# Transposing the residual before its norm is known: the step between the output projection and the feed-forward half of a decoder block

## The chip, the cores and the metric

The kernel runs on one core of one Trainium2 chip. The time is device time in microseconds (us) of one execution on that core, a median over several runs. A core has TensorE (PE, matrix products into PSUM), VectorE (DVE), ScalarE (ACT), GpSimd (POOL) and a queue engine (SP) that issues the loads. Each engine works through its own instructions in order.

## The reference, cut to what matters

One layer of a decoder trunk, 256 tokens, width 2048, feed-forward width 5632, all in float32. The part around the change:

```python
x = x + g1 * y                                       # y: the mixers' outputs @ w_out
h = rmsnorm(x, norm_ffn) * (1.0 + sc2) + sh2         # sc2, sh2: one number for each of the 2048 features
gate = causal_dwconv(h @ w_gate, conv_w) + conv_b
x = x + g2 * ((silu(gate) * (h @ w_up)) @ w_down)
# rmsnorm(x, w) = x * rsqrt(mean(x * x, axis=-1) + 1e-6) * w
```

## The kernel before

Every float32 product of the large matrices is made of three products of rounded parts: a value is split into a high part (`wh`, `Y2[:, k, 0:T]`, `H2[:, k, 0:T]`; ScalarE casts) and a low part (`wl`, the second half of `Y2` or `H2`; VectorE subtracts). Weights come by pieces of 128x1024 (512 KB): a load into one of five buffers `wr`, then the split into one of three buffers `wh` and `wl` (L158). A piece's buffers come free when TensorE is done with it. The order of the instructions on each engine is not written by hand: a scheduler takes the program's order as priority and lets a later instruction go ahead where, by its own model of the times, the earlier ones can't start yet.

**End of the attention half.** The output projection (`project`, L950) works through five chunks of columns; for each of the two token tiles `t` of 128 it sums into one PSUM bank `wot`. Each chunk is then multiplied by the gate `g1` (`m_`, L984), added to the residual `x1` (in the trace: bigC; L985), and squared on ScalarE with a sum by token (`x1s`, L986). In the trace helpers have one line each: L97 is every product (transposes have lines of their own), L100 every two-input VectorE operation, L103 scalar_tensor_tensor, L107 and L109 tensor_scalar, L112 ScalarE's activation, L115 the cast of a split.

**Start of the feed-forward half.** The sums `x1s` give the factor by token `s1` (L996 to L998, the power on GpSimd), and two diagonal matrices `dg` hold it (L1000). For each of 16 tiles `k` of 128 features, two float32 products `x1` times `dg` transpose the residual and scale it by token at once (L1005), into one of eight PSUM banks `fpt`; ScalarE applies scale and shift by feature (`h2`, in the trace h, two buffers; L1007); then the split into `H2` (in the trace bigA; L1008).

**The gate and up projections** (`proj`, L1014) take four `fpt` banks at a time; over the 16 `k` they add, for each of four column tiles, a 512-column product with `wh` and a 256-column product with `wl`. Eleven pairs of such blocks, then the product with `w_down`, fill the rest of the kernel.

Of the kernel before, what the change touches and what calls it, by code (L numbers as in the profile page):

```python
# [16 lines left out]
P = 128  # L17
# [11 lines left out]
# columns of w_in  # L29
# [3 lines left out]
# columns of the constant array  # L33
# [11 lines left out]
# the groups of K tiles in which w_in is worked through: first tile, how many  # L45
GROUPS = ((0, 4), (4, 4), (8, 4), (12, 4))
NG = len(GROUPS)
# how many of the 18 pairs of columns beside DeltaNet's queries, keys and values each group but the last visits
TAKE = (16, 12, 11)
# the order of the mixers: gla, pooling, forgetting attention, DeltaNet  # L50
ORDER = "gpfd"
# modulations (s: scale 2, h: shift 2, g: gate 1; half) summed on the tensor engine and on VectorE, steps per load of columns
# [4 lines left out]
def _consts():  # L57
    i = np.arange(P)
    s, t = i[:, None], i[None, :]
    same = (s // CH) == (t // CH)  # L60
    cols = [s == t, same & (s <= t), same & (s > t), s <= t, np.ones((P, P)), s > t]
    cols.append(np.where(t > s, -1e30, 0.0))
    for w in (2, 4, 8, 16):
        cols.append(np.broadcast_to(1.0 / np.minimum(np.arange(1, 17), w), (P, 16)))
    # the level at which s and t part, counted from 1 above the diagonal and from 7 below it
    lv = sum((l + 1) * ((s // (2 * m) == t // (2 * m)) & (s % (2 * m) < m) & (t % (2 * m) >= m))
             for l, m in enumerate(LEVELS))
    lw = lv.T
    cols.append(lv + np.where(lw > 0, lw + len(LEVELS), 0))
    return np.ascontiguousarray(np.concatenate([np.asarray(a, np.float32) for a in cols], axis=1))  # L70
# [3 lines left out]
def trunk_kernel(ctx: ExitStack, tc: tile.TileContext, x, c, w_mod, b_mod, norm_mix, norm_ffn, w_in,  # L74
# [21 lines left out]
    def mm(o, l, r, start=True, stop=True):  # L96
        PE.matmul(o, lhsT=l, rhs=r, start=start, stop=stop, skip_group_check=True)  # L97
# [30 lines left out]
    # ones in the rows 0 and 64, and in the rows 32 and 96  # L128
# [45 lines left out]
    def gemv(col0, done, pst=None, ready=lambda: True, bias=None):  # L174
        """cond * w over 1024 columns: without pst summed by partition on VectorE, else on the tensor engine,
        four column tiles side by side"""
        acc = pst() if pst else keep.tile([P, 1024], F32, name="ga", tag="ga")
        if bias is not None:
            G.memset(acc, 0.0)
            nc.sync.dma_start(acc[0:1], bias)  # L180
        for k in range(0, KT, 2):
            wms = []
            for kk in range(2):
                wms.append(wp.tile([P, 1024], F32, name="wm", tag="wm", bufs=4))
                last_wm[0] = nc.sync.dma_start(wms[kk], wm_v[:, k + kk, col0:col0 + 1024])
            for kk in range(2):
                wm = wms[kk]
                if not pst:
                    accumulate(acc, wm, k + kk, bias is None)
                    continue  # L190
                for c in range(2):
                    o = 64 * kk + 32 * c
                    mm(acc[o:o + 32], cond[:, k + kk:k + kk + 1].to_broadcast([P, 32]), wm[:, c * 512:c * 512 + 512],
                       start=k == 0, stop=k == KT - 2)
            if k == KT - 2:
                while not ready():
                    yield
                with tc.high_priority():
                    if pst:
                        gr = wp.tile([P, 1024], F32, name="wr", tag="wr", bufs=5)[:, 0:512]  # L200
                        S_.copy(gr, acc)
                        done([(gr, sel[:, c:c + 1]) for c in range(2)])
                    else:
                        done([(acc[:, c * 512:c * 512 + 512], ones) for c in range(2)])
            yield
# [21 lines left out]
    # ================= attention half =================  # L227
    with ExitStack() as ph:
# [11 lines left out]
        # projections: gla q 0:2, k 2:4, g 4:8, gdn g 8:12, pool 12:16, fox q 16:20, k 20:24  # L240
# [16 lines left out]
        def gates():  # L257
# [13 lines left out]
            # columns 0:4 1/(1+e), columns 4:12 1/(2+e)  # L271
# [16 lines left out]
        with ExitStack() as st:  # L288
# [25 lines left out]
            # 1 + b_mod of the two scales  # L314
# [19 lines left out]
            # sh1, sc1 of the K tiles of group g, then h  # L334
# [60 lines left out]
            # the small columns: lr 0:16, b 16:20, a 20:24, f 24:28; row 28 is one  # L395
# [30 lines left out]
            # one pair of column tiles over some groups of K tiles; two sums share a bank: only the first clears it  # L426
# [68 lines left out]
            # g1 takes the place of values no longer needed  # L495
# [33 lines left out]
            # conv of gdn's q, k, v straight from the accumulators  # L529
# [37 lines left out]
        def gated_deltanet():  # L567
            # norms of q and k
# [12 lines left out]
            # decays within the chunk  # L581
# [17 lines left out]
            for t in range(NT):  # L599
                ts = slice(t * P, t * P + P)  # L600
                # exp of the decays, transposed: [j, i], i no earlier than j
# [8 lines left out]
                # -M^T (and its diagonal, which no level takes)  # L610
# [9 lines left out]
            # inverse of I + M by blocks of 2, 4, .. 64: X = inverse, Y = its transpose  # L620
# [30 lines left out]
            for t in range(NT):  # L651
                ts = slice(t * P, t * P + P)
                # keys and values by token
# [9 lines left out]
                # attention [j, i]  # L663
# [5 lines left out]
                # queries times the decay from the chunk's start  # L669
# [6 lines left out]
            # u and w^T, over the values' and the keys' place  # L676
# [10 lines left out]
            # the states, chunk by chunk, over M and X  # L687
# [19 lines left out]
            # outputs, normalised, in place of Y  # L707
            oss, ors = dt_("oss", zz), dt_("ors", zz)
            for t in range(NT):
# [12 lines left out]
                # r = c * (c^2 * ss / d + eps)^-1/2  # L722
# [9 lines left out]
        def finish(on_t, t, nw, i, b):  # L732
            """the gate's place takes the gated output, [features, tokens]"""
            for h in range(4):
                PE.transpose(b[:, h], on_t[:, h], ident)
            o = pr[:, i:i + 4, t * P:t * P + P]
            stt(o, b, nw, o, ALU.mult, ALU.mult)

# [1 line left out]
        def gla(lp):  # L740
# [4 lines left out]
            # log decays by token, then their sums within the chunk by feature  # L745
# [14 lines left out]
            # attention within the chunk, [s, t], heads by parity: the diagonal, then level by level  # L760
# [29 lines left out]
            # to and from the states  # L790
# [159 lines left out]
        def project(n, a):  # L950
            c0, w = chunks[n]
            nk = 1024 // w
            for j in range(KT // nk):
                ks = order[nk * j:nk * j + nk]
                if n == 0:
                    for k in ks:
                        split(Y2[:, k, 0:T], Y2[:, k, T:], pr[:, k + 4])
                wh, wl = load_split(wo_v, ks[0], nk, c0, w)
                for kk, k in enumerate(ks):
                    st, sp_ = j + kk == 0, nk * j + kk == KT - 1  # L960
                    for t in range(NT):
                        xh, xl = Y2[:, k, t * P:t * P + P], Y2[:, k, T + t * P:T + t * P + P]
                        mm(a[t], xh, wh[:, kk], start=st, stop=False)
                        mm(a[t], xh, wl[:, kk], start=False, stop=False)
                        mm(a[t], xl, wh[:, kk], start=False, stop=sp_)
# [22 lines left out]
    # ================= feed-forward half =================  # L988
    with ExitStack() as ph:
# [3 lines left out]
        with tc.tile_pool(name="hp", bufs=2, reuse_waits="tile") as hp:  # L993
            s1 = hp.tile([P, 4], F32, name="s1", bufs=1)
            dg = hp.tile([P, NT, P], F32, name="dg", bufs=1)
            V.tensor_reduce(out=s1[:, 0:2], in_=x1s, axis=AX.X, op=ALU.add)  # L996
# [4 lines left out]
            # transposed and scaled by the norm in one product  # L1001
            for k in range(KT):
                b = fpt()
                for t in range(NT):
                    mm(b[:, t * P:t * P + P], x1[:, t, k * P:k * P + P], dg[:, t])  # L1005
                h = hp.tile([P, T], F32, name="h2", tag="h2", bufs=2)
                act(h, b[:, 0:T], AF.Identity, scale=s2[:, k:k + 1], bias=sh2[:, k:k + 1])  # L1007
                split(H2[:, k, 0:T], H2[:, k, T:], h)  # L1008
# [5 lines left out]
        def proj(gp, view, c0):  # L1014
            """four column tiles, weights stationary: [features, tokens], the high and the low part's sums side by side"""
# [29 lines left out]
        # down: tokens stationary; g2 and the final norm's weight by row  # L1045
# [72 lines left out]
```

## Time and profile before

| | us |
|---|---|
| median of 3 runs | 1316.04 |
| lowest and highest | 1313.96, 1318.38 |
| span of the profiled execution, from its first to its last instruction | 1312.4 |
| TensorE busy in it | 1257.7 (96%) |
| VectorE busy | 886.8 (68%) |
| ScalarE busy | 640.7 (49%) |
| end of the last product of the output projection | 540.54 |
| start of the first product of the gate's projection | 556.71 |

The page tells the profiled execution by its span alone. Times in the trace are us from the span's start. A busy TensorE is not TensorE at its peak: its products are pipelined, their recorded ends overlap the next ones, and its clock has two levels, which the page gives as the granted clock (1.00 is 2.4 GHz, 0.50 is 1.2 GHz).

### The profile page before, as it was taken

Reading aid. Unit: us, or ns where it says so; the run is one execution under the profiler, and the core shown is the slowest. Engines: PE = TensorE matmul, PEld = TensorE weight load, DVE = VectorE, ACT = ScalarE, POOL = GpSimd, SP = SyncE. Lnnn points to the kernel's source line nnn. Section 1 sums busy time; section 2 is a strip of 40 time slices with the busy share of each in tenths; the row PEclk is TensorE's granted clock in tenths of the full one; section 3 lists DMA queues with packets and bytes.
Section 4 is the critical chain, followed back from the end, with each engine's and each line's share of the span. In section 5 each row is a group of like instructions: output and inputs, shape, how many; then the busy total and the mean of one; then the engine's idle time right before and its main releaser. Section 6 shows DMA issues by size and latency. Waiting matters only on the chain.

```text
span 1312.4 us, 20435 instructions
## 1 busy us (share of the span) xinstructions
PE 1257.7 (96%) x7955; PEld 1100.5 (84%) x7955; DVE 886.8 (68%) x1185; ACT 640.7 (49%) x1008; POOL 23.1 (2%) x31
## 2 busy tenths in 40 slices
PE   2799999999999999899999999999999999999996
PEld 1799999898876788888888888888888888888896
DVE  7688797989763497456656665665666587974553
ACT  3455344674364444465545455554555454443432
POOL 0200000010000100000000000000000000000000
PEclk8799999999999999899999999999999999999998
DMA  9999998796567996345565565555655699875552
GB/s 332 287 368 376 312 353 279 259 334 211 176 233 247 328 338 230 125 161 186 170 206 180 189 190 183 190 184 187 191 184 172 206 356 378 304 260 188 192 182 81
DMA packets 174232, 311.95 MB, mean 238 GB/s; under 512 B 16172, under 2 KB 65331, under 8 KB 173495
## 3 DMA queue, kind: packets, MB, share of 16 engines
q1 hardware_dynamic: 174135, 310.65, 70.3%
q8 instruction: 62, 1.02, 0.3%
q14 instruction: 35, 0.29, 0.1%
HBM read 308.51 MB, written 2.10 MB: 237 GB/s over the span
## 4 chain that ended last, share of the span: by engine, by line
PE 91%; DMA 4%; DVE 1%; SPq 1%; ACT 1%; issue 1%; POOLq 0%; POOL 0%; ACTq 0%; DVEq 0%
PE fpt L97 57%; PE ext L97 15%; PE wot L97 5%; PE acc L97 4%; PE gdt L97 4%; PE bgt L97 3%; DMA wm<-in_w_mod_dram 3%; PE oxt L97 2%; DMA wr<-in_w_in_dram 1%; DMA wr<-in_w_out_dram 1%; DVE ga L103 1%; DVE wl L100 0%; ACT h L112 0%; SPq L155 0%; SPq L399 0%
## 5 line engine op out<-in xcount | busy, mean ns | idle before, releaser
L100 DVE TENSOR_TENSOR wl<-wr,wh 128x1024 fp32r<-128x1024 f32 x384 | 468.5, 1223 | 299.7 <-ACT wh L115 298.8
L115 ACT CAST wh<-wr 128x1024 fp32r<-128x1024 f32 x384 | 402.4, 1051 | 497.5 <-PE fpt L97 315.5
L97 PE MATMUL fpt<-bigA,wh 128*128 128x512 f32 x1408 | 485.0, 397 | 0.7 <-ACT h L112 0.7
L97 PE MATMUL fpt<-bigA,wl 128*128 128x256 f32 x1408 | 375.2, 281 | 0.0
L97 PEld LDWEIGHTS fpt<-bigA,wh 128*128 128x128 f32 x1408 | 260.9, 188 | 60.7 <-ACT h L112 0.9
L97 PEld LDWEIGHTS fpt<-bigA,wl 128*128 128x128 f32 x1408 | 259.5, 188 | 5.0
L103 DVE SCALAR_TENSOR_TENSOR ga<-wm,cond,ga 128x1024 f32<-128x1024 f32 x139 | 177.9, 1280 | 9.9 <-DMA wm<-in_w_mod_dram 8.7
L97 PE MATMUL fpt<-wl,AH 128*128 128x512 f32 (+1 forms) x440 | 152.9, 348 | 0.0
L97 PE MATMUL fpt<-wh,AL 128*128 128x512 f32 (+1 forms) x440 | 152.5, 347 | 0.0
L97 PE MATMUL fpt<-wh,AH 128*128 128x512 f32 (+1 forms) x440 | 142.6, 348 | 0.0
L97 PE MATMUL ext<-bigA,wh 128*128 128x256 f32 x768 | 137.9, 281 | 0.0
L97 PEld LDWEIGHTS ext<-bigA,wh 128*128 128x128 f32 x768 | 117.8, 189 | 3.1 <-DVE dS L100 0.8
L97 PE MATMUL ext<-bigA,wl 128*128 128x256 f32 x384 | 107.6, 281 | 1.7 <-DVE wl L100 1.7
L97 PEld LDWEIGHTS fpt<-wh,AH 128*128 128x128 f32 x440 | 83.3, 189 | 10.9 <-ACT wh L115 0.2
L97 PEld LDWEIGHTS fpt<-wh,AL 128*128 128x128 f32 x440 | 83.3, 189 | 10.5 <-issue 0.2
L97 PEld LDWEIGHTS fpt<-wl,AH 128*128 128x128 f32 x440 | 83.3, 189 | 10.5 <-issue 0.2
L97 PEld LDWEIGHTS ext<-bigA,wl 128*128 128x128 f32 x384 | 72.1, 188 | 3.0 <-DVE wl L100 2.1
L97 PE MATMUL acc<-bigA,wh 128*128 128x256 f32 x384 | 69.8, 288 | 4.6 <-ACT bigA L115 2.8
L97 PE MATMUL ext<-wh,bigA 128*128 128x256 f32 (+1 forms) x320 | 68.3, 305 | 0.0
L97 PEld LDWEIGHTS acc<-bigA,wh 128*128 128x128 f32 x384 | 60.1, 196 | 4.9 <-ACT bigA L115 2.9
L97 PE MATMUL wot<-wh,bigA 128*128 128x512 f32 (+1 forms) x256 | 63.0, 337 | 0.0
L97 PEld LDWEIGHTS ext<-wh,bigA 128*128 128x128 f32 x320 | 51.8, 188 | 5.5 <-ACT wh L115 1.7
(335 smaller groups left out, 1193.3 us busy)
## 6 DMA issues: line engine op xcount, KB each, us to landing
wm<-in_w_mod_dram SPq DMA_DIRECT2D x192, 512.0 KB, 6.0
wr<-in_w_in_dram SPq DMA_DIRECT2D x88, 512.0 KB, 9.6
wr<-in_ffn_w_gate_dram SPq DMA_DIRECT2D x88, 512.0 KB, 4.3
wr<-in_ffn_w_up_dram SPq DMA_DIRECT2D x88, 512.0 KB, 3.5
wr<-in_ffn_w_down_dram SPq DMA_DIRECT2D x88, 512.0 KB, 4.5
wr<-in_w_out_dram SPq DMA_DIRECT2D x32, 512.0 KB, 4.1
xt<-in_x_dram SPq DMA_DIRECT2D x2, 1024.0 KB, 7.0
bigC<-in_x_dram SPq DMA_DIRECT2D x2, 1024.0 KB, 11.3
```

The source lines that it names most:

```text
L97: PE.matmul(o, lhsT=l, rhs=r, start=start, stop=stop, skip_group_check=True)
L100: V.tensor_tensor(out=o, in0=a, in1=b, op=op)
L103: V.scalar_tensor_tensor(out=o, in0=a, scalar=s, in1=b, op0=op0, op1=op1)
L115: S_.copy(hi, src)
```

## The change

The products with `dg` go. The residual is transposed as it is, without the norm's factor, two `k` to a PSUM bank, and copied by ScalarE into a new SBUF tile `xT` (16 KB on each partition). The factors by token are brought to all partitions by one small product of `ones` with `dg` into a PSUM bank `R`. VectorE multiplies each `xT[:, k]` by the scale of the feature and by `R`; ScalarE adds the shift and rounds to the high part in one operation; VectorE adds the shift again and takes the high part off, which gives the low part. Beside that, the last piece of the last chunk of the output projection is worked through by token tile: all its products for `t` = 0, then all for `t` = 1.

```diff
                 wh, wl = load_split(wo_v, ks[0], nk, c0, w)
-                for kk, k in enumerate(ks):
+                steps = [(kk, k, t) for kk, k in enumerate(ks) for t in range(NT)]
+                if n == len(chunks) - 1 and ks[-1] == order[-1]:
...
+                    steps.sort(key=lambda s: s[2])
+                for kk, k, t in steps:
                     st, sp_ = j + kk == 0, nk * j + kk == KT - 1
-                    for t in range(NT):
-                        xh, xl = Y2[:, k, t * P:t * P + P], Y2[:, k, T + t * P:T + t * P + P]
-                        mm(a[t], xh, wh[:, kk], start=st, stop=False)
-                        mm(a[t], xh, wl[:, kk], start=False, stop=False)
-                        mm(a[t], xl, wh[:, kk], start=False, stop=sp_)
+                    xh, xl = Y2[:, k, t * P:t * P + P], Y2[:, k, T + t * P:T + t * P + P]
+                    mm(a[t], xh, wh[:, kk], start=st, stop=False)
+                    mm(a[t], xh, wl[:, kk], start=False, stop=False)
+                    mm(a[t], xl, wh[:, kk], start=False, stop=sp_)
...
             dg = hp.tile([P, NT, P], F32, name="dg", bufs=1)
+            xT = hp.tile([P, KT, T], F32, name="xT", bufs=1)
...
             for t in range(NT):
                 tsc(dg[:, t], ident, s1[:, t:t + 1], None, ALU.mult)
...
+            for k in range(0, KT, 2):
+                b = fpt().rearrange("p (k t) -> p k t", t=T)
+                for kk in range(2):
+                    for t in range(NT):
+                        PE.transpose(b[:, kk, t * P:t * P + P], x1[:, t, (k + kk) * P:(k + kk + 1) * P], ident)
+                S_.copy(xT[:, k:k + 2], b)
+
+            R = fpt()[:, 0:T]
+            for t in range(NT):
+                mm(R[:, t * P:t * P + P], ones, dg[:, t])
             for k in range(KT):
-                b = fpt()
-                for t in range(NT):
-                    mm(b[:, t * P:t * P + P], x1[:, t, k * P:k * P + P], dg[:, t])
                 h = hp.tile([P, T], F32, name="h2", tag="h2", bufs=2)
-                act(h, b[:, 0:T], AF.Identity, scale=s2[:, k:k + 1], bias=sh2[:, k:k + 1])
-                split(H2[:, k, 0:T], H2[:, k, T:], h)
+                stt(h, xT[:, k], s2[:, k:k + 1], R, ALU.mult, ALU.mult)
+                act(H2[:, k, 0:T], h, AF.Identity, bias=sh2[:, k:k + 1])
+                stt(H2[:, k, T:], h, sh2[:, k:k + 1], H2[:, k, 0:T].bitcast(F32), ALU.add, ALU.subtract)
```

## Rows read from the trace of the kernel before

**Rows 1.** The page of the profiled execution: its head; busy time, share of the span and count of each engine; the chain that ended last, by engine.

```profile
span 1312.4 us, 20435 instructions
...
PE 1257.7 (96%) x7955; PEld 1100.5 (84%) x7955; DVE 886.8 (68%) x1185; ACT 640.7 (49%) x1008; POOL 23.1 (2%) x31
...
PE 91%; DMA 4%; DVE 1%; SPq 1%; ACT 1%; issue 1%; POOLq 0%; POOL 0%; ACTq 0%; DVEq 0%
```

**Rows 2.** The chain of work that ended last, in order of time, from the end of the output projection to the first products of the gate's projection: start us, us, engine, tile and line.

```profile
527.93 12.26 PE wot L97 x104
...
543.30 0.71 POOL s L998
...
544.03 0.30 DVE dg L107
...
544.37 4.22 PE fpt L97 x18
...
548.62 1.02 ACT h L112 x2
...
556.71 43.49 PE fpt L97 x245
```

**Rows 3.** Windows of the same stretch: length, then for each engine its busy us (instructions that touch the window), the granted TensorE clock, the share of the DMA engines, GB/s.

```profile
core 0: us, PE busy (x) PEld busy (x) DVE busy (x) ACT busy (x) POOL busy (x), PEclk, DMA share, GB/s
...
540.00:544.00 4.00, 0.54 (x5) 0.33 (x3) 2.95 (x8) 1.85 (x5) 0.70 (x1) 0.88 0.51 158
544.00:545.00 1.00, 0.63 (x3) 0.63 (x4) 0.48 (x2) 0.00 (x0) 0.00 (x0) 0.50 0.78 229
...
549.00:550.00 1.00, 1.00 (x8) 1.00 (x7) 0.03 (x1) 1.00 (x4) 0.00 (x0) 0.57 0.00 0
550.00:551.00 1.00, 1.00 (x12) 1.00 (x11) 0.73 (x2) 0.75 (x3) 0.00 (x0) 1.00 0.00 0
...
560.00:570.00 10.00, 10.00 (x59) 8.72 (x58) 5.84 (x9) 7.07 (x12) 0.00 (x0) 1.00 0.29 85
```

**Rows 4.** Timeline of TensorE: start us, us busy, line, operation, output<-inputs, shape, count [idle before <-what ended it].

```profile
540.26 0.28 PE L97 MATMUL wot<-wh,bigA 128*128 128x256 f32 x1
544.37 8.23 PE L97 MATMUL fpt<-dg,bigC 128*128 128x128 f32 x48 [3.84 <-DVE dg L107]
552.97 1.17 PE L97 MATMUL fpt<-dg,bigC 128*128 128x128 f32 x8 [0.36 <-ACT h L112]
...
556.71 0.50 PE L97 MATMUL fpt<-bigA,wh 128*128 128x512 f32 x1 [0.70 <-ACT h L112]
...
557.86 0.40 PE L97 MATMUL fpt<-bigA,wh 128*128 128x512 f32 x1
...
559.27 0.40 PE L97 MATMUL fpt<-bigA,wh 128*128 128x512 f32 x1
```

**Rows 5.** Timeline of ScalarE over the same stretch, same columns.

```profile
540.57 1.04 ACT L115 CAST wh<-wr 128x1024 fp32r<-128x1024 f32 x1 [1.77 <-PE wot L97]
...
541.93 0.40 ACT L112 ACTIVATE m__5606<-bigC 128x256 f32<-128x256 f32 x1
...
548.62 1.02 ACT L112 ACTIVATE h<-fpt,sh,s 128x256 f32<-128x256 f32 x2 [6.20 <-PE fpt L97]
...
562.61 0.40 ACT L115 CAST bigA<-h 128x256 fp32r<-128x256 f32 x1
563.24 1.05 ACT L115 CAST wh<-wr 128x1024 fp32r<-128x1024 f32 x1 [0.23 <-PE fpt L97]
564.19 0.40 ACT L115 CAST bigA<-h 128x256 fp32r<-128x256 f32 x1
```

**Rows 6.** Timeline of VectorE, same columns; the last row is from the end of the first gate and up columns.

```profile
540.22 0.42 DVE L100 TENSOR_TENSOR m__5602<-wot,fv 128x256 f32<-128x256 f32 x1 [0.17 <-PE wot L97]
...
541.65 1.23 DVE L100 TENSOR_TENSOR wl<-wr,wh 128x1024 fp32r<-128x1024 f32 x1
...
565.80 2.35 DVE L100 TENSOR_TENSOR wl<-wr,wh 128x1024 fp32r<-128x1024 f32 x2
...
582.70 0.86 DVE L103 SCALAR_TENSOR_TENSOR cv<-fpt,V,cv 128x255 f32<-128x255 f32 x2
```

**Rows 7.** Transposes elsewhere in this kernel: a group of four in the mixers, and the residual's first transposes at the start of the kernel, before and after 21 us, with the copy that evacuates them (duration ns min/median/max, first and last start us).

```profile
396.60 0.60 PE L656 MATMUL gdt<-ident,bigC 128*128 128x128 f32 x4
...
L327 PE MATMUL ext<-ident,xt x12: 421/421/477, 16.2 to 18.8; 128*128 128x128 f32 x12
...
L327 PE MATMUL ext<-ident,xt x9: 272/273/332, 20.8 to 22.2; 128*128 128x128 f32 x9
...
L328 ACT COPY bigC<-ext x8: 586/586/588, 16.8 to 22.5; 128x512 f32<-128x512 f32 x8
```

**Rows 8.** Groups of TensorE products by line in two windows at either clock (count | busy us, mean ns): the norm's products at 544.2 to 549.4 and at 550 to 556.5.

```profile
L97 PE MATMUL fpt<-dg,bigC 128*128 128x128 f32 x23 | 5.3, 428 | 3.8 <-DVE dg L107 3.8
...
L97 PE MATMUL fpt<-dg,bigC 128*128 128x128 f32 x40 | 5.3, 283 | 1.1 <-ACT h L112 1.1
```

**Rows 9.** Timeline of TensorE early in the kernel, around another pause, and the granted clock of the microseconds there.

```profile
53.34 0.50 PE L97 MATMUL acc<-bigA,wh 128*128 128x256 f32 x2 [1.76 <-ACT wh L115]
...
52.00:53.00 1.00, 0.00 (x0) 0.00 (x0) 0.00 (x0) 0.75 (x1) 0.00 (x0) 1.00 1.00 287
...
55.00:56.00 1.00, 1.00 (x7) 1.00 (x7) 1.00 (x1) 0.00 (x0) 0.00 (x0) 0.50 1.07 406
```

## The prediction, written before the changed kernel was run

> **What bounds the kernel now.** The page comes first: the chain that ended last is TensorE for 91% of the span, VectorE and ScalarE are busy 68% and 49% [rows 1]. A change beside TensorE is therefore worth only what it takes from stretches in which TensorE waits or runs slowly. So the second view is the chain in order of time around the change. There the chain leaves TensorE when the output projection ends, goes through VectorE, GpSimd, TensorE and ScalarE, and comes back to TensorE at 556.71 us for good [rows 2]. The last product of the projection ends at 540.26 + 0.28 = 540.54 [rows 4], so the stage costs 16.17 us. Behind it TensorE is busy 10.00 of 10.00 us at a granted clock of 1.00 [rows 3]: the gate block runs at TensorE's pace, and what starts it earlier shortens the kernel, as long as its operands keep up.
>
> The reader is to see three things in these 16 us. First, TensorE idles 3.84 us for the norm: the power on GpSimd from 543.30, `dg` from 544.03 [rows 2, 4]. Second, its clock fell in that pause and stays at 0.50 (1.2 GHz) until 549.9, by the 0.57 of the microsecond from 549 [rows 3]; a record of the norm's products then takes 428 ns instead of 283 [rows 8]. Third, ScalarE starts `h` only at 548.62, after 18 records of the products [rows 2, 5]. A float32 product leaves two records here, so `k` = 0 alone would need four: the other token tile's products for eight `k` were put ahead. From there the two `h` buffers and the banks set the pace, until the gate block gets its banks at 556.71.
>
> **The change part by part.**
> *The norm's chain* up to `dg` is kept. With the last piece sorted by token tile, one of the two products with `g1`, one addition and one square move ahead of 540.54. What they free is at most two VectorE operations of 0.42 us [rows 6]; but the split of the third gate piece holds VectorE from 541.65 to 542.88 [rows 6], after its cast on ScalarE [rows 5], and the sums follow it. I take 0 (bounds: 0.8 us earlier, or 0.6 later if one copy of 0.586 us [rows 7] goes ahead of the square). `R`'s first product can start at 544.37, like the first product with `dg` today [rows 4].
>
> *The transposes* are 32. A group of four took 0.60 us, with a record of 0.272 [rows 7], so they follow each other by (0.60 - 0.272) / 3 = 0.11 us, together 3.5 us. They need no norm, so they fill the pause from 540.54 to about 544.1 and cost nothing. Without that cover they cost 3.5.
>
> *`R`* is two products, four records. At full clock twelve records touch the microsecond from 550 [rows 3], so one starts every (1.00 + 0.283) / 12 = 0.107 us, and `R` takes 3 x 0.107 + 0.283 = 0.60: done at 545.0; at the low clock (18 records in 4.22 us [rows 2], so 0.21 each) 1.06. I take 545.1, since the second `dg` comes later.
>
> *The first `H2`.* One VectorE multiplication (0.86 us for two of such a form, one operand in PSUM [rows 6], so 0.43), one ScalarE operation (0.40, the cast of the same size [rows 5]), one VectorE operation (0.42 to 0.43 [rows 6]), and some 0.05 us for each of four hand-overs: 1.45 us, so 546.6. ScalarE may be late: from 540.57 it has the cast of 1.04, a square of 0.40 with its read-out of about 0.2 [rows 5], and eight copies of 0.586 [rows 7], together 6.3 us, until 546.9; if all copies stand ahead of the first `hi`, the first `H2` is there at 547.8. I take 547.2 for the gate's start. Its four banks are free, as the copies release them. Gained: 556.71 - 547.2 = 9.5 us.
>
> *The clock.* TensorE would pause from 545 to 547. The bounds are 0, if it stays at full clock, and half of the 5.5 us for which the low level outlasted the work's return today (544.37 to 549.9 [rows 3, 4]), 2.75. Near it lies a pause of 1.76 us before 53.34, after which the clock was at 0.50 from 55 [rows 9]. That speaks for a fall in some phases of the clock and not in others, so I take 1.4. It also matters whether transposes hold the clock. At the start of the kernel TensorE ran transposes alone: twelve took 421 ns each, and from 20.8 us nine took 273 [rows 7], the lengths of low and full clock in this trace [rows 8]. So transposes raised it, and I let them hold it. The Trainium skill, "TensorE: Matmul & The Clock Gate", section "Part 4: PE-mode transpose", states the opposite: the full clock does not engage for transposes, which don't count as a busy engine. Rows 7 don't agree with it; by it the rival below named "cold" would be the forecast.
>
> *The gate block as a new race.* Today all but the last `H2` are done before the fourth weight piece needs its split: the cast of that piece comes at 563.24, ahead of only the last `h` cast [rows 5]. After the change both fall in the same microseconds. A `k` takes TensorE 559.27 - 557.86 = 1.41 us [rows 4], a piece of two `k` 2.82, the block 22.6. VectorE has 32 operations x 0.43 = 13.8 us, and the splits of the five remaining pieces and of two of the next block at 2.35 - 1.23 = 1.12 each [rows 6], 7.8: together 21.6 of the 22.6 + 1.4 us. It fits with little room. What counts is the order. Three pieces are split beforehand, so the fourth is needed 8.5 us after the start, at 555.7. If the scheduler lets its split go between the `H2` operations as its buffers come free, as it did at 563.24, the wait is 0. If it puts it behind all of them, they end at 545.1 + 14.2 = 559.3, cast and split follow until about 561.2, and TensorE waits 5.5. I take 0.8, near the first. The loads, up to five pieces ahead, are late only after that.
>
> *Sum:* 9.5 - 1.4 - 0.8 = 7.3 us less. The profiled execution would go from a span of 1312.4 to 1305.1. The runs shown have a median of 1316.04, 3.6 above that span; the same 7.3 off it gives **1308.7 us**.
>
> **The rivals.**
> *Splits behind the `H2` operations.* As worked out: the fourth piece is split at 561.2; today TensorE reaches it at 556.71 + 8.5 = 565.2. The gain is 4.0, the time 1312.0. For it: `H2` stands earlier in the program. Against: the order at 563.24.
> *Transposes drawn into the projection.* Those of `k` 0 to 13 need only earlier chunks, so the scheduler may put 28 of them between the projection's products. TensorE has no gap there (one unbroken piece of 12.26 us up to 540.2 [rows 2]), so 28 x 0.11 = 3.1 us are paid, the norm comes that much later, and the pause is empty as today. 7.3 - 3.1 = 4.2, less some clock: 1312.0.
> *Cold.* Transposes don't hold the clock: it falls near 543 as today (0.88 over the four us from 540, so 0.96 us at 0.50 [rows 3]), after 22 transposes; ten more at 0.21 end at 545.2, `R` at 546.3, the gate starts at 547.8 and is at full clock 5.5 us after `R` began, at 550.7: 1.5 lost. 556.7 - 547.8 - 1.5 - 0.8 = 6.6, so 1309.4. Rows 7 speak against it; it is the skill's rule just named.
> *VectorE becomes the bound, and the kernel is slower.* With d us for each of the 32 operations and five splits, the last `H2` is ready at 545.1 + 32 d + 5.6, and the block ends 1.4 later; today it ends at 556.71 + 22.6 = 579.3. It decides from d = 0.85 on; at 1.0 the block ends at 584.1, 4.8 later: 1320.8. The row nearest to it has 0.43 [rows 6], and only the first of the two operations reads PSUM.
>
> **How the numbers follow.** Chances: the forecast 0.52, splits behind 0.15, transposes drawn ahead 0.14, cold 0.12, VectorE as bound 0.04, something else that eats the gain 0.03. About 0.3%, 3.9 us, is what a measurement of this kernel can tell from no change. Faster than 1312.1 are nearly all of the forecast and of cold (0.61) and somewhat under half of the two that lie at the bound (0.13): 0.74. Slower is 0.04, the rest, 0.22, is the same. The range: with the earliest start, no clock loss and no wait the gain is 10.1 (1305.9), and the medians scatter by a us or so; the two rivals at 1312.0 belong into it with theirs. 1304.8 to 1313.0 leaves out about 2 in 10.
>
> **What would show it.** Transposes in one run right behind the projection's last product, `R` near 544.4 to 545.1, the first gate product near 547, a granted clock of 0.50 for at most some 3 us then. The fourth piece's cast between `H2` operations, and no wait of TensorE over a us in the gate block, would bear out the last term. The prediction is wrong if the gate starts after 550, if TensorE stands for several us on a `wl` near 556, or if transposes appear before 540.

## The result, and the profile after

| | before | changed |
|---|---|---|
| median, us | 1315.48 (4 runs, 1313.96 to 1318.38) | 1308.03 (4 runs, 1305.91 to 1309.94) |
| ratio to before | | 0.9942, 95% interval 0.9925 to 0.9959 |
| span of the profiled execution, us | 1312.4 | 1304.1 |
| last product of the projection to first product of the gate, us | 16.17 | 6.85 |

1308.7 us was forecast. A second set of runs of the same kernel, on the chip of the last experiments, gave 1309.59 beside 1314.77 for the kernel before (ratio 0.9958, 0.9945 to 0.9972). The two intervals overlap, and the forecast's ratio, 1308.7 / 1316.04 = 0.9944, lies in the first and just under the second.

The page after (head, busy time, the chain by engine): TensorE is still the chain, of a span that is 8.3 us shorter.

```profile
span 1304.1 us, 20373 instructions
...
PE 1251.1 (96%) x7927; PEld 1094.0 (84%) x7927; DVE 893.8 (69%) x1201; ACT 638.1 (49%) x1000; POOL 23.5 (2%) x31
...
PE 92%; DMA 5%; DVE 1%; ACT 1%; issue 1%; SPq 1%; POOLq 0%; ACTq 0%; DVEq 0%
```

The chain around the change, in the columns of [rows 2]:

```profile
524.95 16.39 PE wot L97 x139
...
541.36 1.06 ACT wh L115
542.42 0.40 ACT m__5602 L112 x2
542.83 0.47 ACT xT L1011
543.29 0.41 ACT m__5606 L112 x2
543.70 3.39 ACT xT L1011 x7
547.10 0.42 ACT bigA L112
...
547.54 0.49 DVE bigA L103
...
548.17 51.90 PE fpt L97 x292
```

The projection ends 0.78 us later than before, at 541.32. Stages ahead of the change vary by that much from one execution to the next: in a second profiled execution of the same changed kernel it ends at 542.34. From there to the gate's first product it was VectorE, GpSimd, TensorE and ScalarE [rows 2]; now it is ScalarE nearly throughout: its cast, two squares, and eight copies of the transposed residual (`xT`, L1011) up to 547.10, one of them ahead of the second square; then one high part, one low part on VectorE, and the gate at 548.17. From there TensorE goes on without a recorded pause, here for 51.90 us, to the end of that view.

TensorE's timeline, as [rows 4] (L1010 is the transposes):

```profile
541.16 3.65 PE L1010 MATMUL fpt<-ident,bigC 128*128 128x128 f32 x32
545.41 0.68 PE L97 MATMUL fpt<-dg,ones 128*128 128x128 f32 x4 [0.59 <-DVE dg L107]
548.17 0.47 PE L97 MATMUL fpt<-bigA,wh 128*128 128x512 f32 x1 [2.07 <-DVE bigA L103]
```

The 32 transposes stand right behind the projection's last product and take 3.65 us. The product of the factors begins 0.59 us after them, released by the diagonal matrices, and TensorE then pauses 2.07 us. The windows, columns as in [rows 3], show what the clock did in that pause, just behind it and far behind it:

```profile
547.00:548.00 1.00, 0.00 (x0) 0.00 (x0) 0.47 (x3) 0.90 (x3) 0.00 (x0) 1.00 0.05 20
...
549.00:550.00 1.00, 1.00 (x7) 0.86 (x7) 0.81 (x3) 0.76 (x2) 0.00 (x0) 1.00 0.06 16
...
560.00:570.00 10.00, 10.00 (x58) 8.54 (x57) 8.27 (x14) 5.90 (x9) 0.00 (x0) 1.00 0.61 184
```

It stays at 1.00; in the pause of 3.84 us before it fell to 0.50 [rows 3]. VectorE and ScalarE (columns as in [rows 5, 6]):

```profile
543.74 0.16 DVE L1000 TENSOR_REDUCE s<-x1s 128x2 f32<-128x10 f32 x1
...
544.98 0.48 DVE L107 TENSOR_SCALAR dg<-ident,s 128x128 f32<-128x128 f32 x2 [0.88 <-POOL s L1002]
546.13 0.87 DVE L103 SCALAR_TENSOR_TENSOR h<-xT,s,fpt 128x256 f32<-128x256 f32 x2 [0.67 <-PE fpt L97]
547.54 0.88 DVE L103 SCALAR_TENSOR_TENSOR bigA<-h,sh,bigA 128x256 fp32r<-128x256 f32 x2 [0.53 <-ACT bigA L112]
...
552.28 1.23 DVE L100 TENSOR_TENSOR wl<-wr,wh 128x1024 fp32r<-128x1024 f32 x1
```

```profile
543.61 3.48 ACT L1011 COPY xT<-fpt 128x512 f32<-128x512 f32 x7
546.94 0.96 ACT L112 ACTIVATE bigA<-h,sh 128x256 fp32r<-128x256 f32 x2
...
550.70 0.51 ACT L112 ACTIVATE bigA<-h,sh 128x256 fp32r<-128x256 f32 x1 [0.94 <-DVE h L103]
551.19 1.05 ACT L115 CAST wh<-wr 128x1024 fp32r<-128x1024 f32 x1
552.15 0.90 ACT L112 ACTIVATE bigA<-h,sh 128x256 fp32r<-128x256 f32 x2
```

The two kinds of VectorE operations go at 0.87 and 0.88 us for two, where 0.86 was assumed. The cast of the fourth gate piece (551.19) and its split on VectorE (552.28) stand between the operations that make `H2`, not behind them. From 560 to 570 TensorE is busy 10.00 of 10.00 us, with VectorE at 8.27. From the gate's first product to the end of the span it is 755.93 us, before 1312.44 - 556.71 = 755.7: 0.2 us are given back behind the gate's start. Most of it lies at one place: the product at 565.26 is recorded with 0.50 us instead of 0.40, and the next one starts 0.34 behind it instead of 0.23 or 0.24. VectorE was making a pair of low parts just then, from 564.73 on, so it was probably a short wait for `H2`; the profile doesn't name it.

So 9.32 us gained between projection and gate, 0.2 given back, 0.78 lost ahead of the change: 8.3 in this pair of executions.

### The profile page after: what moved, and what is told of

It is laid out like the page before. It is cut to its first block, busy times and chain, and to the rows that moved or that the text cites. A ratio compares the mean times of both kernels' runs of the same rounds, so it can differ in the third digit from the quotient of the medians.

```text
span 1304.1 us, 20373 instructions
## 1 busy us (share of the span) xinstructions
PE 1251.1 (96%) x7927; PEld 1094.0 (84%) x7927; DVE 893.8 (69%) x1201; ACT 638.1 (49%) x1000; POOL 23.5 (2%) x31
## 4 chain that ended last, share of the span: by engine, by line
PE 92%; DMA 5%; DVE 1%; ACT 1%; issue 1%; SPq 1%; POOLq 0%; ACTq 0%; DVEq 0%
PE fpt L97 57%; PE ext L97 16%; PE wot L97 5%; PE acc L97 4%; PE gdt L97 4%; DMA wm<-in_w_mod_dram 4%; PE bgt L97 3%; PE oxt L97 2%; DVE ga L103 1%; DMA wr<-in_w_in_dram 1%; DMA wsm<-in_w_in_dram 0%; ACT xT L1011 0%; DVE wl L100 0%; ACT wh L115 0%; PE oxt L873 0%
```

## The experiments

Each runs beside the kernel before on the same chip. "Behind" is the time from the projection's last product to the gate's first one in the profiled execution; time lost ahead of the projection's end is not in it, though it is in the medians. "To the end" is from the gate's first product to the end of the span. Both are of one profiled execution.

| kernel | behind | to the end | median | ratio (95% interval) |
|---|---|---|---|---|
| before | 16.17 | 755.7 | | |
| changed | 6.85 | 755.9 | 1308.03 | 0.9942 (0.9925 to 0.9959) |
| changed, again | 6.84 | 758.6 | 1309.59 | 0.9958 (0.9945 to 0.9972) |
| without the sort | 6.85 | 757.4 | 1308.82 | 0.9946 (0.9930 to 0.9961) |
| the sort alone | 16.17 | 755.7 | 1316.53 | 1.0005 (0.9996 to 1.0014) |
| transposes behind the norm | 11.80 | 755.95 | 1313.86 | 0.9983 (0.9972 to 0.9993) |
| transposes as products | 9.38 | 755.9 | 1310.06 | 0.9954 (0.9936 to 0.9971) |
| before, both `dg` in one instruction | 12.77 | 755.7 | 1313.71 | 0.9980 (0.9966 to 0.9994) |
| each transpose four times | 16.22 | 755.9 | 1315.92 | 0.9998 (0.9987 to 1.0010) |
| two copies on VectorE | 6.99 | 757.3 | 1309.35 | 0.9945 (0.9928 to 0.9962) |
| those, third split behind the sums | 7.83 | 758.5 | 1309.13 | 0.9947 (0.9929 to 0.9965) |
| changed, idle transposes in the pause | 6.85 | 755.9 | 1306.12 | 0.9939 (0.9928 to 0.9951) |
| another order | 5.99 | 757.8 | 1307.33 | 0.9942 (0.9930 to 0.9955) |
| another order, idle transposes | 5.99 | 756.2 | 1305.49 | 0.9931 (0.9920 to 0.9943) |

**Without the sort, and the sort alone.**

```diff
-                if n == len(chunks) - 1 and ks[-1] == order[-1]:
-                    steps.sort(key=lambda s: s[2])
```

> The changed kernel without the sort of the projection's last piece by token tile. My theory (the transposes fill the pause, and the gate's banks come free by the copies instead of by the 12 pairs of h): the sort is worth at most 0.4 us, since VectorE's split of the third gate piece stands between the additions and the sums; about 1308.3 us, the gate's first product 6.8 to 7.3 us behind the projection's last (6.8 in the changed kernel). Rival (the sort brings the norm forward and with it everything): 1310 us or more, the gate 8.5 us or more behind.

> The kernel before with only the sort of the projection's last piece. My theory: within 0.5 us of the kernel before, 1315 us; the gate's first product still about 16 us behind the projection's last. Rival (the sort is part of the gain): 2 us or more faster.

The sort is worth nothing that shows, alone or with the rest: 6.85 us behind without it, 16.17 behind with nothing else. What it frees on VectorE ends in the same wait for ScalarE's cast and the split of the third gate piece.

**When the transposes run.** The identity is made anew from the second diagonal matrix, so the transposes wait for the norm:

```diff
+            id2 = hp.tile([P, P], F32, name="id2", bufs=1)
+            tsc(id2, dg[:, 1], 0.0, None, ALU.is_gt)
...
-                        PE.transpose(b[:, kk, t * P:t * P + P], x1[:, t, (k + kk) * P:(k + kk + 1) * P], ident)
+                        PE.transpose(b[:, kk, t * P:t * P + P], x1[:, t, (k + kk) * P:(k + kk + 1) * P], id2)
```

> The changed kernel, but the transposes use an identity that VectorE makes from the second diagonal matrix, so that they wait for the norm. My theory: TensorE idles 4 us again, its clock falls to 0.50, the transposes run from 4.4 us behind the projection on and take 3.5 us at full or 6.8 at the low clock, the product of the factors stands behind them; the gate starts 11 to 14 us behind the projection's last product instead of 6.8, so 4 to 7 us of the gain go: 1312 to 1315 us. Rival (the gain comes from the copies that free the banks, and when the transposes run doesn't matter): 1308 us.

TensorE's timeline there, and two windows:

```profile
549.04 5.26 PE L1012 MATMUL fpt<-id,bigC 128*128 128x128 f32 x32 [4.29 <-DVE id L107]
...
556.55 0.47 PE L97 MATMUL fpt<-bigA,wh 128*128 128x512 f32 x1 [1.79 <-DVE bigA L103]
...
550.00:551.00 1.00, 1.00 (x6) 1.00 (x5) 0.00 (x0) 0.59 (x1) 0.00 (x0) 0.50 0.14 53
...
552.00:553.00 1.00, 1.00 (x10) 1.00 (x9) 0.00 (x0) 0.89 (x2) 0.00 (x0) 0.87 0.00 0
```

A pause of 4.29 us is back, the clock falls, and the transposes take 5.26 us instead of 3.65; the gate starts 11.80 us behind. So 11.80 - 6.85 = 4.95 of the 9.32 us hang on transposing before the norm is known; about 0.3 of them are the making of the identity, which the changed kernel doesn't have. The ratio is 0.9983 against 0.9942, and the intervals don't overlap.

**What covers them.** The transposes as products with the identity, and each of them four times over:

```diff
-                        PE.transpose(b[:, kk, t * P:t * P + P], x1[:, t, (k + kk) * P:(k + kk + 1) * P], ident)
+                        mm(b[:, kk, t * P:t * P + P], x1[:, t, (k + kk) * P:(k + kk + 1) * P], ident)
```

> The changed kernel with the 32 transposes made as float32 products with the identity (two records each). My theory: they start at the same place and take 64 x 0.107 = 6.8 us at full clock, 3.3 more than the pause covers; the product of the factors ends 7.5 us behind the projection, the gate starts 8.9 behind instead of 6.8: 1310 us. Rival (ScalarE's copies set the gate's start anyway): no change, 1308 us.

```diff
-                        PE.transpose(b[:, kk, t * P:t * P + P], x1[:, t, (k + kk) * P:(k + kk + 1) * P], ident)
+                        for _ in range(4):
+                            PE.transpose(b[:, kk, t * P:t * P + P], x1[:, t, (k + kk) * P:(k + kk + 1) * P], ident)
```

> The changed kernel with each of the 32 transposes made four times over into the same place. It tells two things: what transposes cost when nothing covers them, and whether transposes alone hold the clock. My theory (they hold it): 128 x 0.11 = 14.1 us at a granted clock of 1.00 throughout, the gate starts 14.1 + 0.7 + 1.45 = 16.3 us behind the projection's last product instead of 6.8, so 1317.5 us. Rival (transposes don't count): the clock falls to 0.50 within 4 us of the first transpose, the later ones follow each other by 0.21 us, and the gate starts 24 us or more behind: 1325 us or more.

The chain with products:

```profile
524.90 18.26 PE wot L97 x155
543.16 7.61 PE fpt L97 x68
...
552.54 12.48 PE fpt L97 x69
```

The 64 records and the four of the factors' product take 7.61 us and stand on the chain without a pause; the norm is no longer on it, and the gate starts 9.38 behind (8.9 was worked out: from the factors' product to the gate it is 552.54 - 550.77 = 1.77 us, not 1.45). With four times the transposes, the chain, the transposes by line (duration ns min/median/max, first and last start) and one window:

```profile
539.98 13.97 PE fpt L1011 x128
...
556.20 5.89 PE fpt L97 x32
...
L1011 PE MATMUL fpt<-ident,bigC x128: 271/273/273, 539.8 to 553.7; 128*128 128x128 f32 x128
...
551.00:553.00 2.00, 2.00 (x21) 2.00 (x19) 0.00 (x0) 0.67 (x2) 0.00 (x0) 1.00 0.00 0
```

13.97 us of nothing but transposes stay at a granted clock of 1.00, each 273 ns. Transposes held the clock here. They raised it in the kernel with the late transposes: its granted clock goes from 0.50 to 1.00 in the microsecond from 552, while TensorE does nothing else, and their records from 421 ns to 273, the two lengths of the start of the kernel [rows 7]. So the rule of the Trainium skill, "TensorE: Matmul & The Clock Gate", section "Part 4: PE-mode transpose", that they don't count, doesn't hold for these. Beyond the pause transposes cost nearly their full time: 96 more put the gate 16.22 - 6.85 = 9.37 us later, 0.10 each (16.3 behind was worked out; the median is 1315.92, 1317.5 was expected).

**How much was only the order.** Both diagonal matrices in one VectorE instruction, in the kernel before:

```diff
-            for t in range(NT):
-                tsc(dg[:, t], ident, s1[:, t:t + 1], None, ALU.mult)
+            tt(dg, ident[:, None, :].broadcast_to([P, NT, P]), s1[:, 0:2].unsqueeze(2).broadcast_to([P, NT, P]), ALU.mult)
```

> The kernel before, with both diagonal matrices made by one VectorE instruction, so that no token tile's products can go ahead of the other's. Reading of the trace of before: ScalarE's first h waits 3.2 us longer than its own two products, since one token tile's products of eight tiles k stand ahead. My theory: the first h comes about 1 us behind the first product at the low clock instead of 4.2, the rest of the chain of h keeps its pace, and the gate starts 3 us earlier: 1313 us, some third of the changed kernel's gain. Rival (the banks and the chain of h set the gate's start whatever the order): no change, 1316 us.

ScalarE's first `h`, and TensorE:

```profile
545.37 0.57 ACT L112 ACTIVATE h<-fpt,sh,s 128x256 f32<-128x256 f32 x1 [2.91 <-PE fpt L97]
...
544.54 9.04 PE L97 MATMUL fpt<-dg,bigC 128*128 128x128 f32 x64 [3.98 <-DVE dg L100]
553.33 0.48 PE L97 MATMUL fpt<-bigA,wh 128*128 128x512 f32 x1
```

The first `h` starts 0.83 us behind the first product instead of 4.25, and the gate follows the 64 records without a wait: 12.77 us behind. A third of the gain, 16.17 - 12.77 = 3.40 us, could have been had in the old form (by the median, 1316.11 - 1313.71 = 2.4 us on that chip). The late transposes are another 12.77 - 11.80 = 0.97 ahead of it, as a balance: TensorE's work from its first record to the end of the factors' product is 5.71 us there, 8.79 here up to the gate; a wait of 1.80 for the first `H2` and a start 0.31 later are taken off that.

**Making the first `H2` sooner.** Two copies on VectorE, and with them the third piece's split (which held VectorE until 543.69) queued behind the sums (`lsq` is the last square, `lrd` the sums; `g` is 2 in the first gate block):

```diff
-                S_.copy(xT[:, k:k + 2], b)
+                if k in (6, 10):
+                    V.tensor_copy(out=xT[:, k:k + 2], in_=b)
+                else:
+                    S_.copy(xT[:, k:k + 2], b)
```

> The changed kernel with two of the eight copies to xT on VectorE (which stands idle for the power and for the product of the factors) instead of ScalarE. In the trace of the changed kernel the chain runs through ScalarE's copies until its first high part at 547.10. My theory: that part comes 0.6 to 1.0 us earlier, then bound by VectorE's first multiplication: 1307.3 us, the gate 6.0 us behind the projection's last product instead of 6.8. Rival (VectorE's copies delay the diagonal matrices or the multiplications as much): no change.

```diff
...
+                if view is wg_v and c0 == 0 and g == 2:
+                    with tc.issue_after(lsq.ins), tc.issue_after(lrd.ins):
+                        wh, wl = load_split(view, 2 * g, 2, c0, 512)
```

> The same two copies on VectorE, and the third gate piece's split is queued behind the last square on ScalarE and behind the sums on VectorE. My theory: the sums come 0.6 us earlier and the first multiplication with them, the gate starts 5.3 us behind the projection's last product: 1306.6 us, 1.5 us less than the changed kernel. Rival (the late split makes TensorE wait for the third piece, which is needed 5.7 us behind the gate's start): no gain over the changed kernel, or a loss.

Both miss. The chain of the second shows why:

```profile
544.44 0.17 DVE s L1000
...
544.72 0.68 DVE xT L1012
545.40 1.20 DVE wl L100
546.60 0.60 DVE xT L1012
547.20 0.21 DVE dg L107
```

VectorE's queue now holds a copy, the split and another copy between the sums (544.44) and the diagonal matrices (547.20). The edit allows the split from the sums on; it was the scheduler that put all three ahead of `dg`. From the sums to `dg` it is 2.76 us, in the changed kernel 544.98 - 543.74 = 1.24; the gate starts 7.83 us behind. Nor do the sums come 0.6 us earlier, but 0.1: they start 2.31 us behind the projection instead of 2.42, since a copy still stands ahead of the second square on ScalarE. In the first kernel a copy between the sums and their scaling does the same in small (6.99).

**The clock in the pause.** In several of these kernels the way "to the end" is 1.4 to 2.7 us longer than 755.9, though TensorE is never recorded idle there. The changed kernel once more, as it is:

> The changed kernel as it is, on the chip and beside the runs of the three kernels that follow. It tells how often TensorE's clock falls in the pause between the product of the factors and the gate. My theory (the loss by the clock is 0 in some executions and 1.5 us or more in others): a median of 1308 to 1309.5 us; the profiled execution either ends about 755.9 us after the gate's first product, with no low stretch there, or about 757.4, with one. Rival (the clock always holds): every profiled execution of it ends 755.9 after.

The gate's first product, and its windows:

```profile
549.18 0.76 PE L97 MATMUL fpt<-bigA,wh 128*128 128x512 f32 x1 [2.07 <-DVE bigA L103]
...
547.00:548.00 1.00, 0.11 (x2) 0.00 (x0) 0.85 (x2) 1.00 (x4) 0.00 (x0) 1.00 0.78 303
548.00:549.00 1.00, 0.00 (x0) 0.00 (x0) 0.47 (x3) 0.92 (x3) 0.00 (x0) 0.73 0.00 0
...
550.00:551.00 1.00, 1.00 (x4) 0.83 (x4) 0.81 (x3) 0.77 (x2) 0.00 (x0) 0.50 0.06 16
...
555.00:556.00 1.00, 1.00 (x7) 0.91 (x6) 0.41 (x1) 1.00 (x3) 0.00 (x0) 0.86 0.00 0
```

The same kernel, the same pause of 2.07 us, but this time the clock falls at 548.5 and stays at 0.50 until 555.3: 758.6 us to the end instead of 755.9, 2.7 lost. The median, 1309.59, lies just above what was expected. Without the sort the clock fell at 549.3, a microsecond after the gate's start, and was back at 552.3; 1.5 us were lost. So the same pause cost something in one execution and nothing in another; what decides between them isn't shown, and one profiled execution of each kernel doesn't tell how often it happens. Idle transposes in the pause (`lr` is the product of the factors):

```diff
...
+            fl = fpt()
+            with tc.issue_after(lr.ins):
+                for i in range(16):
+                    PE.transpose(fl[:, i % 4 * P:i % 4 * P + P], x1[:, 0, 0:P], ident)
```

> The changed kernel with 16 transposes of one tile, whose result nobody reads, behind the product of the factors, so that TensorE works through most of the pause before the gate. My theory: the clock holds at 1.00 in the pause, the gate starts 6.85 us behind the projection's last product as before, and the median is lower by the share of executions that lost 1.5 us: 0.5 to 1 us under the changed kernel. Rival (transposes don't hold the clock, or the filler delays the gate): no gain, or 0.3 us or more of delay of the gate.

```profile
545.24 0.68 PE L97 MATMUL fpt<-dg,ones 128*128 128x128 f32 x4 [0.59 <-DVE dg L107]
545.76 1.91 PE L1019 MATMUL fpt<-ident,bigC 128*128 128x128 f32 x16
548.00 0.47 PE L97 MATMUL fpt<-bigA,wh 128*128 128x512 f32 x1 [0.33 <-DVE bigA L103]
...
549.00:550.00 1.00, 1.00 (x7) 0.91 (x6) 0.81 (x3) 0.58 (x2) 0.00 (x0) 1.00 0.00 0
```

The clock is at 1.00 at the gate's start, and the gate starts no later. The median is 1306.12 against 1309.59 on the same chip, 3.5 us less, where 0.5 to 1 had been expected. The intervals of the two ratios overlap slightly, so the size is not settled. It is more than the 2.7 us that the low stretch cost, so part of it probably comes from elsewhere: in the two profiled executions the projection ends at 542.34 and 541.15. And the way to the end, 755.9, is that of one execution; that the clock holds in every one isn't shown.

**Another order.** All copies behind the last square; two on VectorE, one behind the sums and one behind the diagonal matrices; the third piece's split behind the second pair of high and low parts; then the same with 12 idle transposes (`lts` scales the sums, `ldg` is the second `dg`, `hi1` and `lo1` the parts of `k` = 1):

```diff
...
+                if k in (4, 12):
+                    with tc.issue_after((lts if k == 4 else ldg).ins):
+                        V.tensor_copy(out=xT[:, k:k + 2], in_=b)
+                else:
+                    with tc.issue_after(lsq.ins):
+                        S_.copy(xT[:, k:k + 2], b)
...
+                    with tc.issue_after(hi1.ins), tc.issue_after(lo1.ins):
+                        wh, wl = load_split(view, 2 * g, 2, c0, 512)
```

> The changed kernel with another order: all copies to xT behind the last square, two of them on VectorE (one behind the sums, where it waits for the power, one behind the diagonal matrices, where it waits for the product), and the third gate piece's split behind the second pair of high and low parts. My theory: sums 0.5 us earlier, no engine's copies ahead of the first high part, the gate 5.8 us behind the projection's last product instead of 6.85; about 1 us under the changed kernel. Rival (the third piece's split comes too late): TensorE waits for its low part in the gate block, gate to end longer than 755.9 us at full clock.

> The order of the kernel before this, with 12 such idle transposes behind the product of the factors. My theory: gate 5.8 us behind, no low stretch of the clock, 1.5 to 2 us under the changed kernel: 1306.5 to 1307 us. Rival: as for the two kernels that it joins.

The chain of the second:

```profile
541.94 3.49 PE fpt L1010 x32
...
545.45 0.70 PE fpt L97 x4
...
546.24 0.49 DVE h L103
```

The sums come 0.6 us sooner, and now the transposes themselves (3.49 us of the chain) stand ahead of the factors' product: their cover is used up. The gate starts at 547.93, 5.99 us behind (5.8 was expected). Without the idle transposes its profiled execution had a low stretch too, 757.8 to the end. With them it is 756.2 at full clock, 0.3 longer than in the changed kernel, so the later split of the third piece may cost a little. The kernel has the lowest median of all, 1305.49; its ratio's interval, 0.9920 to 0.9943, lies just below that of the changed kernel on the same chip, 0.9945 to 0.9972, but overlaps that of its first runs, 0.9925 to 0.9959.

## Why the prediction was right, step by step

- **The place and the bound.** Right: what starts the gate block earlier came off the end, us for us, with 0.2 us given back, as long as the clock holds.
- **Transposes in the pause at no cost.** Right: 3.65 us against 3.5, directly behind the projection, and the experiment that puts them behind the norm loses 4.95 us between projection and gate. The product of the factors came 0.59 us after them, so the cover was nearly used up.
- **The norm's chain kept.** Nearly right at 0: the factors' product began 4.09 us behind the projection's last product, the first product with `dg` 3.83 before, so 0.26 later. The sort gave nothing: of what it was to move ahead of the projection's end, one product with `g1` did move (540.76), the addition and the square did not. A copy did go ahead of the second square, the case priced at 0.6; VectorE's split ended at the same time as that square (543.69 and 543.70), so the copy cost little.
- **The first `H2`.** 9.5 us were forecast for the earlier start, 9.32 measured. The 547.2 was a choice between two bounds, 6.06 and 7.26 us behind the projection for the gate. What happened is the later one: all eight copies stand ahead of the first high part. It came at 6.85 instead of 7.26 because the copies follow each other by (3.48 - 0.56) / 6 = 0.49 us, not by their length of 0.586; that outweighs the second square, which the forecast had put ahead of the projection's end. The earlier bound was too early: from the end of the factors' product VectorE's way to the gate takes 1.77 us where nothing else holds it (the kernel with the transposes as products), not 1.45. That the middle of two mis-sized bounds lay so near is partly luck.
- **The clock, 1.4 between 0 and 2.75.** The bounds were right, and the middle is what neither profiled execution of the changed kernel shows: 0 in one, 2.7 in the other. The sign that was set, at most some 3 us at 0.50, held in the first alone; in the second it was 6.8 us. "Cold" is excluded: transposes hold the clock.
- **Weight splits, 0.8.** Too high: TensorE waited for no split in the gate block, and 0.2 us are lost in all, probably to a late `H2`. The scheduler put the splits between, as the cast at 563.24 had suggested [rows 5].
- **The sum.** 7.3 us forecast, 7.45 between the medians. In the pair of profiled executions the terms were 9.32, 0 and 0.2; that the sum agrees more closely than the terms is partly luck, and the second set of runs lay 5.2 us under the kernel before.
- **The rivals.** None of them happened: no transposes before 541.16, no wait for a split, VectorE at 0.43 us an operation. What the list lacked was the cheaper way to a third of the gain: the trace of before had been read rightly (18 records where four would do), and one instruction in place of two removes it.

## What to carry to other kernels

Work that doesn't need a late scalar belongs ahead of it: a transpose can run before the norm is known, if the factor can be applied afterwards on an engine with room, and it is free only as long as the pause lasts (here 3.65 us of transposes in 4.09; 96 more cost 0.10 us each). When a chain of waits shows far more products ahead of a reader than it needs, look at the order in the queue before changing the algorithm. And what a scheduler puts into an idle moment of an engine can stand ahead of the very instruction that the chain waits for.

## What the runs showed of the hardware that was not expected

A pause of TensorE of 2.07 us, with 0.68 us of work and a pause of 0.59 ahead of it, let the clock fall in one profiled execution of a kernel and not in another; the price was 0 or 2.7 us. In seven variants with a pause of 1.73 to 2.08 us ahead of the gate it was 1.4 to 2.6 us in four and nothing in three. Two of these had the same pause, 1.80 us, and no idle time of TensorE between the projection and the factors' product: each transpose four times lost nothing, the other order 1.9. And the granted clock of a trace's first microseconds can't be read as it stands: a window of the kernel before says 1.00 (columns as in [rows 3])

```profile
16.00:17.00 1.00, 1.00 (x5) 1.00 (x6) 1.00 (x1) 0.16 (x1) 0.00 (x0) 1.00 1.04 383
```

while the transposes of that window have the duration of the low clock, 421 ns [rows 7].
